# Expert weights of a decoder layer laid over partitions as 8p+k, so that a load reads 8 KB of a partition in one piece

## The chip, the cores and the metric

The kernel runs on one core of one Trainium2 chip. The metric is the device time of one execution in microseconds, the median of several runs. The engines are named as in the profile: PE is TensorE (PEld its weight loads), DVE is VectorE, ACT is ScalarE, POOL is GpSimd, SP is SyncE, whose queue (SPq) issues every DMA of this kernel. The DMA of a core is done by 16 DMA engines.

## The reference, cut to what matters

One decoder layer over 256 tokens of 1024 channels. A token mixer (sparse attention and an RWKV-7 recurrence) comes first, then a mixture of experts. Only the second half matters for the change:

```
# xt: (256 tokens, 1024 channels), after RMSNorm, scale s2 and shift sh2
# routing: best of 4 groups, best two of its 8 experts -> combine (256, 32)
def body(acc, ew):
    wg, wu, wd, cw = ew                      # (1024, 512), (1024, 512), (512, 1024), all float32
    hdn = jax.nn.silu(xt @ wg) * (xt @ wu)
    return acc + cw[:, None] * (hdn @ wd), None
acc, _ = lax.scan(body, zeros, (w_gate, w_up, w_down, combine.T))   # 32 experts
```

Each expert has 6 MB of weights, the 32 together 192 MB (here 1 MB is 1024 KB). Every expert is computed, on at most 32 of its tokens (a loop for experts with more tokens stands at the end).

## The kernel before, in words

**The weight stream.** A list `loads` holds every weight load of the program in order. For expert e it has two loads of the gate matrix (`eg`), two of the up matrix (`eu`) and then two of the down matrix of the expert before (`ed`), 1 MB each. `pump()` issues them in this order on SP's queue. Each load needs a free place of 2048 columns in SBUF: in the big tile `arena`, or in one of two tiles that appear later, `more_3006` (one place) and `more` (8192 columns, four places). `more` takes the room of the tile `split`, which holds the split operands of the output projection. Where no place is free, `pump` stops until `done()` frees one, and SP then waits for the engine that reads the old contents last.

**How rows lie.** A weight matrix is read as `(k p) n -> p k n`: row 128k+p lies on partition p in block k. A gate load of 1 MB takes four blocks, so that each partition gets four rows of 512 floats that lie 256 KB apart in memory: 4 pieces of 2 KB. A down load takes 512 of 1024 columns of four rows: again 4 pieces of 2 KB.

**The stages.** Up to about 313 us of the profile the token mixer runs. Then the output projection goes over 8 blocks of channels (line 1474 on); each block is 24 matmuls of split operands (`mm3`, lines 517 to 519), a residual add on DVE (1487), and, two blocks later, the router's sums `logits` (1462, 1464). `turn` (1470, 1471) then transposes each block on PE and copies it back to SBUF on ACT. The routing is a chain of small DVE instructions (1529 to 1579). `group` and `gather` (1593) collect the tokens of four experts at a time. For each expert `gate_up` (1618) multiplies into four row groups, ACT copies the result (1619), `hidden` (1625 to 1631) makes the SwiGLU, `down` (1637, 1638) multiplies with half of the columns of the down weights and scales on DVE, and `finish` (1658) adds to the tokens' sums in PSUM. The last expert's `finish` also adds the residual (1660) and sends the output out (1662). While the loop of expert e runs, `down` and `finish` are those of expert e-1. In the loop `done()` gives the four gate and up places back after `gate_up`, and each down place after its `down`.

Of the kernel before, what the change touches and what calls it, by code (L numbers as in the profile page):

```python
# [19 lines left out]
T = 256  # L20
# [55 lines left out]
class Arena:  # L76
    """Columns of one SBUF tile, handed out in program order from the smallest gap that holds them."""
# [11 lines left out]
    def alloc(self, cols, lo=0, hi=None, from_top=True):  # L89
        """a place that has been free for a while if there is one, in the smallest gap"""  # L90
# [65 lines left out]
def layer_kernel(tc, I, out, dbg=None):  # L156
# [17 lines left out]
    # operands in float32r: those that live to the end of the output projection, and those that live up to it  # L174
# [22 lines left out]
    # ---------------------------------------------------------------- weight stream  # L197
# [98 lines left out]
    # ---------------------------------------------------------------- small inputs  # L296
# [29 lines left out]
    # ---------------------------------------------------------------- constants  # L326
# [18 lines left out]
    def rsqrt_steps(dst, src, mul, eps, z, u):  # L345
        """dst = (src * mul + eps) ** -0.5 for a few columns, by Newton steps from a guess out of the exponent"""
# [17 lines left out]
    # ---------------------------------------------------------------- silu(c), x norm  # L364
# [24 lines left out]
    # ---------------------------------------------------------------- modulation rows  # L389
# [6 lines left out]
    def mod_cols(row, gs):  # L396
        """channel-major [128, 8] of the pairs of groups from each of gs on"""
# [11 lines left out]
    def mod_bcast(o, row, g0, mul):  # L409
        """o [128, 1024] = the row of the groups g0, g0 + 1 on every partition, times mul"""  # L410
# [10 lines left out]
    def mod_half(hf):  # L421
        """shift and scale for half of the channels, in four groups: shift and scale, even and odd blocks of rows"""
# [35 lines left out]
        # the vector engine reads one PSUM bank while the scalar engine reads the other  # L458
# [15 lines left out]
    def after_last(f, keep=True):  # L474
        """f(); with keep, the tensor engine's part of it after that of the call before"""
# [9 lines left out]
    def step(it, keep):  # L485
        """the next step of a stream"""
# [6 lines left out]
    # ---------------------------------------------------------------- input projection  # L493
# [3 lines left out]
    def split(w, p=None):  # L497
        """w (512 columns) as a float32r part and the float32r rest"""
# [11 lines left out]
    # the first blocks of weights are split before the activations are there  # L510
# [4 lines left out]
    def mm3(ps, l, r, start, stop):  # L515
        """the product of two split operands, all terms that float32 holds"""
# [4 lines left out]
    def proj_cols(key, c0, ps, last=False):  # L521
        """ps [128, T]: the columns c0 to c0 + 127 of a weight times the split activations"""
# [13 lines left out]
    def shift_mix(dst, ps, i, m=128):  # L536
        """dst = p + (previous p - p) * mu along the tokens"""
# [4 lines left out]
    def rows_part(key, hf, mp, n, fin, i0=0):  # L542
        """n blocks of columns of a weight from block 2 mp on, by half of the rows, into fin(block, their products)"""
# [74 lines left out]
    def rwkv():  # L618
        # ---------------------------------------------------------------- RWKV: decay, a, gate, kk
# [14 lines left out]
        def weave(a, b):  # L634
            """the steps of both, by turns"""
# [36 lines left out]
        # cumulative log decay within a chunk  # L672
# [1169 lines left out]
```

## Time and profile before

| | us |
|---|---|
| median of 3 runs | 833.31 (832.91 to 834.92) |
| profiled execution, first to last instruction (span) | 831.9 |
| what lies around the span, if the profiled execution took the median | 1.4 |

The profiled execution has no time of its own beside its span, so the 1.4 us are the median less the span. The page shows PE busy for 85% of the span, DVE 47%, ACT 24% and POOL 26%, and 261.46 MB moved by DMA, of which 201.3 MB (192 loads of 1 MB as above) are expert weights. A busy share is an average over stages: a matmul that waits in a full pipeline also counts as busy.

### The profile page before, as it was taken

How to read it: one execution, taken by the hardware profiler on the slowest of the kernel's cores; microseconds unless marked ns; L12 is line 12 of the kernel's file. 1: busy time of each engine (PE TensorE's matmuls, PEld its weight loads, DVE VectorE, ACT ScalarE, POOL GpSimd, SP SyncE). 2: the span in 40 equal slices, each digit the busy share in tenths (PEclk: the TensorE clock that was granted, in tenths of full speed). 3: DMA queues.
4: the chain of work that ended last, by engine and by line, in shares of the span. 5: the costliest groups of instructions: out<-in, count | busy, mean ns of one | idle time of the engine just before them, and what ended most of it. 6: DMA issues, size and time to landing. Idle time of an engine off the chain costs nothing.

```text
span 831.9 us, 12649 instructions
## 1 busy us (share of the span) xinstructions
PE 710.2 (85%) x4981; PEld 410.8 (49%) x4981; DVE 387.8 (47%) x861; ACT 201.2 (24%) x438; POOL 216.3 (26%) x251
## 2 busy tenths in 40 slices
PE   5898767899899999899996988888797897798777
PEld 2786556568789899644442332332242242242222
DVE  2577899999857674342337321221131132122113
ACT  2476512434364433211110010010010010010000
POOL 1348758323924156011110010010010001001000
PEclk9899779999999999899999899998999999999899
DMA  9994504557678579699999999999999999999993
GB/s 336 387 301 143 180 23 159 202 176 270 220 262 256 202 254 333 229 376 386 386 386 386 387 387 387 386 387 386 387 387 386 387 387 387 387 386 387 387 386 147
DMA packets 135597, 261.46 MB, mean 314 GB/s; under 512 B 7760, under 2 KB 23120, under 8 KB 133488
## 3 DMA queue, kind: packets, MB, share of 16 engines
q1 hardware_dynamic: 135536, 260.63, 86.9%
q8 instruction: 40, 0.66, 0.3%
q14 instruction: 21, 0.17, 0.1%
HBM read 259.57 MB, written 1.05 MB: 313 GB/s over the span
## 4 chain that ended last, share of the span: by engine, by line
PE 47%; DMA 26%; DVE 15%; SPq 5%; POOL 4%; issue 2%; ACT 1%; POOLq 0%; DVEq 0%
DMA arena<-in_expert_w_up_dram 16%; PE ps_e L1618 10%; DMA more<-in_expert_w_up_dram 7%; PE acc L1658 7%; SPq L280 5%; PE ps_e L1637 4%; PE ps_a L551 3%; PE ps_e L1593 2%; PE ps_g L517 2%; PE ps_e L1625 2%; PE ps_g L519 2%; PE ps_g L518 2%; DVE split L507 2%; DMA arena<-in_expert_w_down_dram 2%; DVE arena L1345 2%
## 5 line engine op out<-in xcount | busy, mean ns | idle before, releaser
L1638 DVE TENSOR_TENSOR arena<-ps_e,arena 128x512 f32<-128x512 f32 x64 | 44.3, 692 | 304.5 <-PE ps_e L1637 304.5
L1618 PE MATMUL ps_e<-arena 128*32 128x512 f32 x784 | 148.8, 661 | 33.6 <-DMA arena<-in_expert_w_up_dram 33.6
L1607 POOL TENSOR_SCALAR arena<-arena 128x128 f32<-128x128 f32 x64 | 51.6, 812 | 410.6 <-PE ps_e L1609 278.9
L1658 PE MATMUL acc<-arena 128*128 128x512 f32 x256 | 123.4, 609 | 24.9 <-DVE arena L1638 24.9
L1618 PEld LDWEIGHTS ps_e<-arena 128*32 128x32 f32 x784 | 32.2, 118 | 124.9 <-issue 65.9
L1658 PEld LDWEIGHTS acc<-arena 128*128 128x128 f32 x256 | 44.6, 192 | 83.2 <-issue 60.7
L507 DVE TENSOR_TENSOR split<-arena,split 128x512 fp32r<-128x512 f32 x84 | 67.1, 808 | 22.9 <-POOL split L504 11.2
L1619 ACT COPY arena<-ps_e 128x512 f32<-128x512 f32 x32 | 18.8, 586 | 241.0 <-PE ps_e L1618 241.0
L1618 PE MATMUL ps_e<-more,arena 128*32 128x512 f32 x240 | 68.0, 619 | 9.9 <-DMA more<-in_expert_w_up_dram 9.9
L504 POOL TENSOR_SCALAR split<-arena 128x512 fp32r<-128x512 f32 x50 | 40.3, 809 | 98.2 <-PE ps_g L518 31.8
L1637 PE MATMUL ps_e<-arena 128*32 128x512 f32 x392 | 62.8, 610 | 0.3 <-DMA arena<-in_expert_w_down_dram 0.3
L551 PE MATMUL ps_a<-split 128*128 128x256 f32 x360 | 50.0, 298 | 3.3 <-ACT split L463 1.9
L551 PEld LDWEIGHTS ps_a<-split 128*128 128x128 f32 x360 | 46.5, 200 | 9.9 <-issue 4.3
L1625 PEld LDWEIGHTS ps_e<-arena 128*128 128x128 f32 x256 | 31.1, 191 | 27.3 <-issue 21.4
L519 PE MATMUL ps_a<-split 128*128 128x256 f32 (+1 forms) x112 | 36.7, 328 | 8.8 <-DVE split L507 4.5
L506 ACT CAST split<-arena 128x512 fp32r<-128x512 f32 x60 | 36.5, 615 | 31.7 <-PE ps_g L518 18.3
L1627 ACT ACTIVATE arena<-ps_e 128x128 f32<-128x128 f32 x32 | 8.9, 278 | 141.7 <-PE ps_e L1625 141.7
L507 POOL TENSOR_TENSOR split<-arena,split 128x512 fp32r<-128x512 f32 x26 | 36.2, 1395 | 13.4 <-ACT split L506 9.6
L517 PE MATMUL ps_g<-split 128*128 128x256 f32 x128 | 38.8, 303 | 0.0
L518 PE MATMUL ps_a<-split 128*128 128x256 f32 (+1 forms) x112 | 35.6, 318 | 2.6 <-POOL split L507 1.0
L519 PE MATMUL ps_g<-split 128*128 128x256 f32 x128 | 36.4, 285 | 1.6 <-DVE split L507 1.6
L517 PE MATMUL ps_a<-split 128*128 128x256 f32 (+1 forms) x112 | 36.0, 326 | 1.8 <-ACT split L506 0.8
(349 smaller groups left out, 1246.1 us busy)
## 6 DMA issues: line engine op xcount, KB each, us to landing
arena<-in_expert_w_gate_dram SPq DMA_DIRECT2D x51, 1024.0 KB, 14.3
arena<-in_expert_w_down_dram SPq DMA_DIRECT2D x49, 1024.0 KB, 14.4
arena<-in_expert_w_up_dram SPq DMA_DIRECT2D x47, 1024.0 KB, 14.3
arena<-in_w_in_dram SPq DMA_DIRECT2D x18, 1024.0 KB, 8.7
more<-in_expert_w_up_dram SPq DMA_DIRECT2D x17, 1024.0 KB, 14.3
arena<-in_ada_w_dram SPq DMA_DIRECT2D x16, 1024.0 KB, 6.4
more<-in_expert_w_down_dram SPq DMA_DIRECT2D x15, 1024.0 KB, 14.3
more<-in_expert_w_gate_dram SPq DMA_DIRECT2D x13, 1024.0 KB, 14.4
```

Of the source, the lines that this page charges most:

```text
L280: nc.sync.dma_start(out=dst, in_=src)
L507: (nc.gpsimd if p[1] == "P" else nc.vector).tensor_sub(l, w, h.bitcast(F32))
L517: nc.tensor.matmul(ps, l[0], r[0], start=start, stop=False)
L518: nc.tensor.matmul(ps, l[0], r[1], start=False, stop=False)
L519: nc.tensor.matmul(ps, l[1], r[0], start=False, stop=stop)
L551: nc.tensor.matmul(p, a[:, kk, :], b[:, 4 * hf + kk, :], start=(i == 0 and kk == KORD[0]), stop=(i == 2 and kk == KORD[-1]))
L1607: nc.gpsimd.tensor_scalar(o4[:, a], io1[:, None, :].to_broadcast([128, 4, CAP]), rk_(a), cb(a), op0=OP.is_equal, op1=OP.mult)
L1618: nc.tensor.matmul(ps[32 * g:32 * g + 32, :], xg[:, kk, :], w[:, k, :], start=(k == 0), stop=(k == 3))
L1625: nc.tensor.matmul(ps[:, 64 * f:64 * f + 64], gu[:, 128 * f:128 * f + 128], SEL, start=True, stop=True)
L1637: nc.tensor.matmul(ps[32 * f:32 * f + 32, 0:n], hT[:, f, :], wd[:, f, :], start=True, stop=True)
L1638: nc.vector.tensor_mul(Y4b[:, s:s + n], ps[:, 0:n], gt2[0][:, s:s + n])
L1658: nc.tensor.matmul(o, stb[e % 2][:, a, :], Y4b[:, s:s + n], start=(e == 0), stop=(e == NE - 1))
```

## The change

The rows of an expert's gate and up matrices are laid over partitions as 8p+k, those of the down matrix as 4p+j. A gate or up load then reads four rows that follow each other in memory, 8 KB in one piece, on each partition; the pieces of neighbouring partitions begin 16 KB apart. A down load takes two whole rows of 1024 floats, also 8 KB in one piece. Only the two loads of the last expert's down matrix stay halves by columns (4 pieces of 2 KB).

What the new order of rows needs elsewhere:

- The channels of the tokens must lie as 8p+k. `turn` writes the transposed blocks to a new tile `h2` (2048 columns, a place of `more`) instead of back into `h`; the 8 copies on ACT have the same number of elements in another order. `h` is freed behind them.
- The scale and shift of the tokens (`s2c`, `sh2`) must follow. `reorder`, placed in the output projection behind the matmuls of block 1, does that with 16 matmuls of 8 columns, a 1024-column copy and four small instructions on DVE.
- The hidden channels must lie as 4p+j: the copy of `gate_up`'s result reads PSUM with a step of 4 elements.
- `down` takes both halves of the hidden channels at once and uses two PSUM tiles; the last expert keeps the form by columns as `down_cols`.
- The residual add of the last `finish` reads `h2` with a step of 128 elements.

```diff
-            w = I[name][0, e].rearrange("(k p) n -> p k n", p=128)
+            w = I[name][0, e].rearrange("(p k) n -> p k n", p=128)
             for i in range(2):
                 add_load((n, e, i), (4, 512), [(None, w[:, 4 * i:4 * i + 4, :])])
         if e:
-            w = I["expert_w_down"][0, e - 1].rearrange("(k p) n -> p k n", p=128)
-            for s, n in ((0, 512), (512, 512)):
-                add_load(("ed", e - 1, s), (4, n), [(None, w[:, :, s:s + n])])
+            w = I["expert_w_down"][0, e - 1].rearrange("(p k) n -> p k n", p=128)
+            for i in range(2):
+                if e < NE:
+                    add_load(("ed", e - 1, i), (2, 1024), [(None, w[:, 2 * i:2 * i + 2, :])])
+                else:
+                    add_load(("ed", e - 1, i), (4, 512), [(None, w[:, :, 512 * i:512 * i + 512])])
...
-        nc.scalar.copy(h[:, m, :], pst[:, 0:256])
+        nc.scalar.copy(h2[:, :, :, 16 * m:16 * m + 16], pst[:, 0:256].rearrange("p (a c k) -> p a k c", a=2, k=8))
+
+    blk, both = M(8), M(2, 8)
+
+    def reorder():
+        nc.vector.tensor_reduce(blk, ident.rearrange("p (m q) -> p m q", m=8), axis=AX.X, op=OP.add)
+        pick = M(8, 8, 16)
+        nc.vector.tensor_copy(pick, ident.rearrange("p (q k) -> p k q", k=8)[:, :, None, :].to_broadcast([128, 8, 8, 16]))
+        ps = PS("g")
+        for k in range(8):
+            for o, v in enumerate((sh2, s2c)):
+                nc.tensor.matmul(ps[:, 64 * o + 8 * k:64 * o + 8 * k + 8], pick[:, k].rearrange("p m q -> p (m q)"), v,
+                                 start=True, stop=True)
+        t = M(2, 8, 8)
+        pv = ps[:, 0:128].rearrange("p (o k m) -> p o k m", o=2, k=8)
+        for o in range(2):
+            nc.vector.tensor_mul(t[:, o], pv[:, o], blk[:, None, :].to_broadcast([128, 8, 8]))
+        nc.vector.tensor_reduce(both, t, axis=AX.X, op=OP.add)
+        A.free(t, blk, pick)
...
+        if j and m == 1:
+            after_last(lambda: None, False)
+            after_last(reorder)
...
+    fr.__exit__(None, None, None)
+    state["more"].append(Arena(pool(name="sb2", bufs=1).tile([128, nB], F32, name="more"), nB))
+    h2 = state["more"][-1].get(2048, from_top=False).rearrange("p (a k c) -> p a k c", a=2, k=8)
     for m in range(8):
         turn(m)
-    fr.__exit__(None, None, None)
-    state["more"].append(Arena(pool(name="sb2", bufs=1).tile([128, nB], F32, name="more"), nB))
+    A.free(h, sh2, s2c)
+    sh2, s2c = both[:, 0], both[:, 1]
...
-        nc.scalar.copy(GUb, ps)
+        nc.scalar.copy(GUb.rearrange("p (j q) -> p j q", j=4), ps.rearrange("p (q j) -> p j q", j=4))
...
-    def down(hT, wd, s, n):
+    def down(hT, wds, then=lambda i: None):
+
+        ps = [PS(), PS()]
+        for i, wd in enumerate(wds):
+            for c in range(2):
+                for j in range(2):
+                    g = 2 * (c ^ i) + j
+                    nc.tensor.matmul(ps[c][32 * g:32 * g + 32, :], hT[:, 2 * i + j, :], wd[:, j, 512 * c:512 * c + 512],
+                                     start=True, stop=True)
+            then(i)
+        for c in range(2):
+            s = slice(512 * c, 512 * c + 512)
+            nc.vector.tensor_mul(Y4b[:, s], ps[c], gt2[0][:, s])
```

**SP's queue, the loads around the routing.** The names are destination and source of a load; `more_3006` and `more` are the two late tiles. Before, the last expert loads ahead of the first expert's `gate_up` and the first ones behind it:

```order
L280 DMA arena<-in_expert_w_gate_dram 128x4x512 x2
L280 DMA more<-in_expert_w_up_dram 128x4x512 x2
L280 DMA more<-in_expert_w_down_dram 128x4x512 x2
L280 DMA arena<-in_expert_w_gate_dram 128x4x512 x2
L280 DMA arena<-in_expert_w_up_dram 128x4x512 x2
```

The same stretch of the change:

```order
L283 DMA arena<-in_expert_w_gate_dram 128x2048 x2
L283 DMA more<-in_expert_w_up_dram 128x2048 x2
L283 DMA more<-in_expert_w_down_dram 128x2048
L283 DMA arena<-in_expert_w_down_dram 128x2048
L283 DMA arena<-in_expert_w_gate_dram 128x2048 x2
```

The shape of a load goes from 4 rows of 512 on each partition to one run of 2048. `h2` has taken one of the four places of `more`, so the second down load goes to `arena` instead, into the place of the first expert's second gate load, and stands behind that expert's `gate_up`.

**PE, the output projection.** Line 1462 is the router's sums, 517 to 519 are the matmuls of split operands. Before, between blocks 1 and 2:

```order
L517 MATMUL ps_a<-split 128x256
L518 MATMUL ps_a<-split 128x256
L519 MATMUL ps_a<-split 128x256
L1462 MATMUL ps_r<-arena 128x36 x2
L517 MATMUL ps_a<-split 128x256
```

The place of the change where the 16 matmuls stand (lines 517 to 519 are 520 to 522 here):

```order
L521 MATMUL ps_a<-split 128x256
L522 MATMUL ps_a<-split 128x256
L1485 MATMUL ps_g<-arena 128x8 x16
L520 MATMUL ps_a<-split 128x256
L521 MATMUL ps_a<-split 128x256
```

They stand between the last product of block 1 and the second half of block 2, 12 matmuls ahead of the router's first sums; nothing else on PE moves in this stage.

**PE, the end of the program.** Line 1618 is `gate_up` of the last expert, 1637 `down`, 1625 `hidden`, 1609 the scatter weights, 1658 `finish`. Before:

```order
L1618 MATMUL ps_e<-arena 32x512 x16
L1637 MATMUL ps_e<-arena 32x512 x4
L1625 MATMUL ps_e<-arena 128x64 x4
L1609 MATMUL ps_e<-arena 128x128 x2
L1637 MATMUL ps_e<-arena 32x512 x4
L1658 MATMUL acc_3389<-arena 128x512
L1658 MATMUL acc_3391<-arena 128x512
L1637 MATMUL ps_e<-arena 32x512 x4
```

The change:

```order
L1645 MATMUL ps_e<-arena 32x512 x16
L1667 MATMUL ps_e<-arena 32x512 x8
L1652 MATMUL ps_e<-arena 128x64 x4
L1636 MATMUL ps_e<-arena 128x128 x2
L1699 MATMUL acc_3410<-arena 128x512
L1699 MATMUL acc_3412<-arena 128x512
L1678 MATMUL ps_e<-arena 32x512 x4
```

The eight `down` matmuls of expert 30 stand together now, ahead of `hidden`; the number of matmuls from `gate_up` to the end is the same.

## Rows read from the trace of the kernel before

**Rows 1.** The page, part 2: DMA share and rate in 40 equal slices

```profile
DMA  9994504557678579699999999999999999999993
GB/s 336 387 301 143 180 23 159 202 176 270 220 262 256 202 254 333 229 376 386 386 386 386 387 387 387 386 387 386 387 387 386 387 387 387 387 386 387 387 386 147
```

**Rows 2.** Busy time by stage, one stage of the experts; last three columns: clock, DMA share, GB/s

```profile
430.00:808.00 378.00, 310.88 (x1710) 116.38 (x1702) 96.35 (x204) 35.92 (x91) 38.70 (x48) 0.95 1.05 387
```

**Rows 3.** The chain that ended last, in order of time: start, length, what

```profile
375.24 3.57 PE ps_e L1593 x32
...
388.79 3.57 PE ps_e L1618 x32
...
398.78 3.57 PE ps_e L1618 x32
...
529.73 3.19 PE ps_e L1618 x25
...
808.75 4.62 PE ps_e L1618 x25
```

**Rows 4.** Timeline of SP's queue around the routing: start, length, issue

```profile
334.19 0.93 SPq L280 DMA_DIRECT2D more<-in_expert_w_up_dram  x2
335.17 1.61 SPq L280 DMA_DIRECT2D more<-in_expert_w_down_dram  x2
352.35 0.92 SPq L280 DMA_DIRECT2D arena<-in_expert_w_gate_dram  x2
```

**Rows 5.** DMA issues in 220 to 345 us: expert loads, KB each, us to landing

```profile
arena<-in_expert_w_gate_dram SPq DMA_DIRECT2D x8, 1024.0 KB, 6.4
arena<-in_expert_w_up_dram SPq DMA_DIRECT2D x5, 1024.0 KB, 5.6
arena<-in_expert_w_down_dram SPq DMA_DIRECT2D x4, 1024.0 KB, 10.5
...
more<-in_expert_w_up_dram SPq DMA_DIRECT2D x3, 1024.0 KB, 8.0
...
more<-in_expert_w_down_dram SPq DMA_DIRECT2D x2, 1024.0 KB, 11.8
```

**Rows 6.** DMA share and rate in 340 to 360 us, 40 slices of 0.5 us

```profile
DMA  9999999999999930000000000009489999999999
GB/s 401 414 406 406 401 397 393 389 389 385 381 381 389 356 115 0 0 0 0 0 0 0 0 0 0 0 8 102 164 332 401 389 381 373 397 389 344 414 414 393
```

**Rows 7.** Busy time by stage, two short stages; last three columns: clock, DMA share, GB/s

```profile
90.00:93.00 3.00, 0.95 (x6) 0.54 (x5) 3.00 (x5) 1.47 (x3) 3.00 (x3) 1.00 1.02 431
94.00:96.00 2.00, 0.23 (x1) 0.23 (x2) 2.00 (x3) 0.92 (x2) 2.00 (x2) 0.71 1.05 404
```

**Rows 8.** DMA issues in 86 to 98 us

```profile
arena<-in_ada_w_dram SPq DMA_DIRECT2D x2, 1024.0 KB, 5.8
arena<-in_w_in_dram SPq DMA_DIRECT2D x1, 1024.0 KB, 9.1
```

**Rows 9.** The chain again, in the output projection

```profile
320.88 0.37 PE ps_r L1462 x4
...
336.23 0.58 PE ps_r L1464 x6
```

**Rows 10.** Groups by line (page, part 5): mean of one in ns, idle before

```profile
L1638 DVE TENSOR_TENSOR arena<-ps_e,arena 128x512 f32<-128x512 f32 x64 | 44.3, 692 | 304.5 <-PE ps_e L1637 304.5
```

**Rows 11.** Timeline of ACT and DVE in the routing

```profile
338.86 0.65 ACT L1471 COPY arena<-ps_g 128x256 f32<-128x256 f32 x2 [0.25 <-PE ps_g L1470]
...
340.43 0.53 ACT L1573 ACTIVATE arena<-arena 128x32 f32<-128x32 f32 x2
...
341.35 0.19 DVE L1575 CUSTOM_DVE_ANT_0 arena<-arena 128x32 f32<-128x32 f32 x1 [0.34 <-POOL arena L1567]
```

**Rows 12.** Timeline of the end

```profile
821.67 1.07 PE L1637 MATMUL ps_e<-arena 128*32 128x512 f32 x8
...
826.40 0.69 DVE L1660 TENSOR_TENSOR arena<-acc,arena 128x512 f32<-128x512 f32 x1 [0.17 <-PE acc L1658]
```

More of the change, by code (lines that the diff above doesn't have):

```diff
@@ L1592, in gather @@
                 for a in range(2):
-                    nc.tensor.matmul(ps[:, n * kk:n * kk + n], h[:, 2 * k2 + kk, 128 * a:128 * a + 128], oh(a), start=(a == 0),
+                    nc.tensor.matmul(ps[:, n * kk:n * kk + n], h2[:, a, 2 * k2 + kk, :], oh(a), start=(a == 0),
                                      stop=(a == 1))
@@ L1631, in hidden, with down_cols @@
         nc.vector.tensor_mul(hT, pv[:, :, 1, :], sg[:, 0])
-    def down(hT, wd, s, n):
+    def down(hT, wds, then=lambda i: None):
[10 more added lines that the diff above has]
+            nc.vector.tensor_mul(Y4b[:, s], ps[c], gt2[0][:, s])
+    def down_cols(hT, wd, s):
         ps = PS()
         for f in range(4):
-            nc.tensor.matmul(ps[32 * f:32 * f + 32, 0:n], hT[:, f, :], wd[:, f, :], start=True, stop=True)
-        nc.vector.tensor_mul(Y4b[:, s:s + n], ps[:, 0:n], gt2[0][:, s:s + n])
+            nc.tensor.matmul(ps[32 * f:32 * f + 32, :], hT[:, f, :], wd[:, f, :], start=True, stop=True)
+        nc.vector.tensor_mul(Y4b[:, s:s + 512], ps, gt2[0][:, s:s + 512])
     pctx.__exit__(None, None, None)
@@ L1659, in finish @@
             if e == NE - 1:
-                nc.vector.tensor_add(y[:, a, s:s + n].rearrange("p (k n) -> p k n", n=128), o.rearrange("p (k n) -> p k n", n=128),
-                                     h[:, s // 128:(s + n) // 128, 128 * a:128 * a + 128])
+                nc.vector.tensor_add(y[:, a, s:s + n].rearrange("p (c k) -> p c k", k=8), o.rearrange("p (c k) -> p c k", k=8),
+                                     h2[:, a, :, s // 8:(s + n) // 8].rearrange("p k c -> p c k"))
                 nc.sync.dma_start(out=out[0, 128 * a:128 * a + 128, s:s + n], in_=y[:, a, s:s + n])
@@ L1687, in layer_kernel @@
             break
-        for c in (0, 512) if e else ():
-            down(hTb, need(("ed", e - 1, c)), c, 512)
-            done(("ed", e - 1, c))
+        if e:
+            down(hTb, [need(("ed", e - 1, i)) for i in range(2)], lambda i: done(("ed", e - 1, i)))
         hidden(hTb)
@@ L1699, in layer_kernel @@
             overflow_tables(nc, ovm, PS(), sel, rk, comb, ones, io)
-    parts = [(e, c) for e in (NE - 2, NE - 1) for c in (0, 512)]
     last[0] = None
-    for i, (e, c) in enumerate(parts):
-        after_last(lambda: down(hTb if e < NE - 1 else hT2, need(("ed", e, c)), c, 512))
-        done(("ed", e, c))
-        if i == 0:
-            after_last(lambda: hidden(hT2))
-            e = NE - 1
-            after_last(lambda: scatter_weights(stb[e % 2], o4b, lambda a: rk[:, a, e:e + 1], lambda a: comb[:, a, e:e + 1]))
-        else:
-            after_last(lambda: finish(*parts[i - 1], 512))
-    after_last(lambda: finish(*parts[-1], 512))
+    e = NE - 1
+    after_last(lambda: down(hTb, [need(("ed", e - 1, i)) for i in range(2)], lambda i: done(("ed", e - 1, i))))
+    after_last(lambda: hidden(hT2))
+    after_last(lambda: scatter_weights(stb[e % 2], o4b, lambda a: rk[:, a, e:e + 1], lambda a: comb[:, a, e:e + 1]))
+    after_last(lambda: finish(e - 1, 0, 512))
+    for i in range(2):
+        after_last(lambda: down_cols(hT2, need(("ed", e, i)), 512 * i))
+        done(("ed", e, i))
+        after_last(lambda: finish(*((e, 0) if i else (e - 1, 512)), 512))
+    after_last(lambda: finish(e, 512, 512))
     ovr, ovw, ovi = ovm[6:]
@@ L1723, in layer_kernel @@
             for t, n in zip(wts, ("expert_w_gate", "expert_w_up", "expert_w_down")):
[L1724 removed]
+                nc.sync.dma_start(out=t, in_=I[n][0, ds(eid, 1)].rearrange("o (p k) n -> p (o k) n", p=128))
             nc.vector.tensor_copy(rw[:, 0], ovr[:, :, ds(i, 1)].rearrange("p a o -> p (a o)"))
@@ L1731, in layer_kernel @@
             hidden(hTb)
-            for c in (0, 512):
-                down(hTb, wts[2][:, :, c:c + 512], c, 512)
+            down(hTb, [wts[2][:, 2 * j:2 * j + 2, :] for j in range(2)])
             scatter_weights(stb[0], o4b, lambda a: rw[:, 0, a:a + 1], lambda a: rw[:, 1, a:a + 1])
```

1 line of the change is left out of this document (removed).

## The prediction, written before the result was known

> **What bounds the kernel now.** I first read the rate of the DMA over the span [rows 1]. Up to slice 17 it moves between 23 and 387 GB/s; in slices 19 to 39, some 437 us, it stands at 386 or 387. The row of the stage from 430 us on says the same: 387 GB/s at a DMA share of 1.05, so the engines' transfers lie end to end [rows 2]. Then the chain in order of time [rows 3]. Around 390 us its pieces are PE's: the `gate_up` of one expert starts at 388.79, the next at 398.78, so PE needs 9.99 us for an expert, and 3.57 us more at every fourth for the `gather` (line 1593), 10.9 us on average. Later each long piece ahead of a `gate_up` is the DMA of its last up load. `gate_up` starts at 529.73 and, 17 experts on, at 808.75: 279.0 / 17 = 16.41 us for six loads, **2.735 us for a load of 1 MB**. The DMA is thus slower than PE by half, and the end is set by how many loads are left when the expert stage begins, and by the pace of one.
>
> When does the stage begin? SP's queue shows the last loads ahead of it at 334.19 and 335.17, and the next at 352.35 [rows 4]; the issues of 220 to 345 us count 8 + 5 + 4 + 3 + 2 = 22 expert loads [rows 5]. These fill every free place. The DMA then has nothing to do: its rate is zero from about 347.5 us on until the first `gate_up` gives places back at 352.35 [rows 6]. So whatever delays that `gate_up` delays the whole stream behind it, one for one, and loads that come earlier ahead of 347 us win nothing.
>
> The sum of before: 192 loads, of which the last four are the down matrices of experts 30 and 31. Up to the last up load 188 - 22 = 166 loads come after 352.35. 166 x 2.735 = 454.0; it lands at 808.75, 456.4 us later, so 2.4 us are the first transfer's start. From there to the end of the span 831.9 - 808.75 = 23.15 us, PE's chain through the last expert; 1.4 us lie around the span: 833.3, the median.
>
> **The change part by part.**
>
> *The pace of a load.* This trace has loads in pieces of 8 KB already: at 87 us two loads of `in_ada_w`, 2048 columns of one row for each partition, with a load of `in_w_in` in 2 KB pieces (4 rows of 512) behind them [rows 8]. In the 3 us in which only the first two run, the rate is 431 GB/s; in the 2 us of the third it is 404 [rows 7]. Two readings: taken as it is, 431 against the 387 of the long stage; or, since 2 KB pieces also run at 404 in so short a stretch and at 387 in a long one (the slices from 340 us on fall the same way, from 414 to 381), the long stage keeps the ratio, 387 x 431 / 404 = 413. I take the middle, **422**: both ends come from one pair of rows, and neither is nearer. A load then takes 2.735 x 387 / 422 = 2.508 us (2.456 to 2.563).
>
> The Trainium skill, "DMA: Bandwidth & Descriptors", section "Why small descriptors are slow (HBM only)", says that every packet costs some 3 cycles beside its 32-byte beats. A piece of 2 KB would then go from 67 to 64.75 cycles for each 2 KB, 3.5%, and the whole would come to about 824 us. The pair of rows shows 6.7% between the two sizes, so the trace does not agree with so small a cost.
>
> *One load more.* `h2` takes one of the four places of `more`, and `h`'s room, freed, makes no other place: SP's order shows the second down load of expert 2 behind the first `gate_up`. 21 loads lie ahead, 167 follow: 2.5 us.
>
> *`reorder`.* PE sits in the output projection without a gap and on the chain. Of the nearest row, the router's sums, four entries (two matmuls of 36 columns) take 0.37 us, and six of one column 0.58 [rows 9]: 0.19 us a matmul whatever the columns, two entries each. 16 x 0.19 = **3.0 us** on the path. On DVE a copy of 1024 columns is about twice a 512-column instruction of 692 ns [rows 10], 1.4 us, placed in the branch projection, ahead of what makes the splits that PE waits for; between nothing and 1.4 I take 0.5. The four small DVE instructions lie beside PE's 3 us. Together 3.5 us (bounds 2.5 to 5.5).
>
> *`turn`.* Eight copies on ACT, 0.65 us a pair, the last ending at 339.5; then the exponentials (0.53), which end at 340.96, and DVE takes their result at 341.35 [rows 11]: 0.4 us of cover, and then the routing, on the path, waits. Nothing in the trace shows a copy with this order of elements. The number of elements is the same; I take nothing, and as the other bound 2 us (each copy longer by 0.25 us), which the 5.5 above includes.
>
> *The order of `gate_up`'s copy, `down`, `finish`.* Up to 430 us PE's work is hidden behind the DMA's backlog, later behind its pace: 10.9 us of work against 15.05. Uncovered is only the end. There the same matmuls stand in another order, and the last add on DVE (0.69 us) reads with a step: nothing, or one more 0.69 [rows 12]. The last four loads come 2 x 2.51 + 2 x 2.735 = 10.5 us after the last up load, and PE wants the last of them at 821.67 - 808.75 = 12.9 us: 2.4 us of cover; I leave 23.15 as it is.
>
> **The sum.** 352.35 + 3.5 = 355.85; + 2.4 + 167 x 2.508 (418.8) = 777.05; + 23.15 = 800.2 of span; + 1.4 = **801.6, said as 802**. The bounds of the pace give 793 and 811, those of the rest move this by 1 down and 3 up: 792 to 814.
>
> **The rivals.**
>
> *The long pieces help only up to the short-stretch rate.* If what slows 2 KB pieces from 404 to 387 in a long run is their number alone, and nothing is won beyond, the pace is 2.735 x 387 / 404 = 2.62 us and the time 801.6 + 18.7 = 820. For it: 404 is the one rate that 2 KB pieces have reached. Against: the 431 beside it. This is also where the skill's rule above ends.
>
> *The memory sets the pace, not the pieces.* 387 stands to within one GB/s for 437 us, as a fixed limit would. Then 167 x 2.735 = 456.7, and with the 3.5 us of `reorder` and the added load the time is 839.5: slower. It decides where the pace stays over (454.0 - 3.5) / 167 = 2.698 us, a rate under 392. Against: 404 and 431 in the same trace, and a share of 1.05 in the DMA's own rows. The skill's "DMA: Bandwidth & Descriptors", section "Where 436 GB/s comes from", holds that memory binds loads at about 358 GB/s a core; the 387 of this trace is above that already, so it can't be the limit here.
>
> *The new addresses collide.* The pieces of neighbouring partitions begin 16 KB apart, a power of two, where those of `in_ada_w` are 24 KB apart; the trace has no long load with such a step. At 360 GB/s a load takes 2.94 us, and the time is 874.
>
> *PE becomes the bound.* It needs 10.9 us against 15.05 an expert. Only a clock that falls by a quarter closes that; the stage shows 0.95 [rows 2]. Then some 833.
>
> **How the numbers follow.** My forecast 0.66, the short-stretch rate 0.16, the memory's limit 0.09, PE as the bound or a mixture that eats the gain 0.05, collisions 0.04. The range for 8 in 10 reaches from 789 (a pace a little under the lower bound) to 823, with the first rival in it; the likeliest case alone has 792 to 814. A difference of 0.3% (2.5 us) is about what a measurement of this kernel can tell from none: under 830.8 is faster, with the first two cases and a part of the mixture, 0.86; same 0.04; slower 0.10, the memory's limit and the collisions less a little.
>
> **What the profile would show.** Rate of the long stage: 413 to 431 says the step on the pace is right, 404 the first rival, 387 the second, less the third. The share of DMA should be near 1 again. Six loads: about 15.05 us between two `gate_up` of the DMA-bound stretch. The gap of the DMA ahead of the first `gate_up` should grow (the loads end earlier), and the first issue behind it should come at 355 to 358. The chain's late pieces should still be up loads; if they are PE's, PE has become the bound. Wrong would make me above all a rate that falls over a long run more for long pieces than for short ones, or copies of `turn` far longer than 0.35 us.

## The result, and the profile after

| | before | after |
|---|---|---|
| median | 834.12 us (832.91 to 839.86) | 805.76 us (803.52 to 808.79, 4 runs) |
| profiled execution: time | not given | 806.51 us |
| its span | 831.9 us | 804.7 us |

The ratio is 0.9654 with a 95% interval of 0.9601 to 0.9706: faster, 28 us. The forecast was 802 us in a range of 789 to 823.

The changed kernel's page, part 2 (40 slices of the span) and its packets, answers to [rows 1]; the last line is the packets of before:

```profile
DMA  9995414456788566649999999999999999999994
GB/s 334 386 302 182 157 53 131 144 211 213 260 283 286 198 235 248 231 165 407 421 421 420 422 421 421 419 421 421 421 421 420 423 420 421 421 420 422 420 418 155
DMA packets 62636, 261.45 MB, mean 325 GB/s; under 512 B 7760, under 2 KB 23120, under 8 KB 36208
...
DMA packets 135597, 261.46 MB, mean 314 GB/s; under 512 B 7760, under 2 KB 23120, under 8 KB 133488
```

The same megabytes go in fewer than half of the packets, and the long stage, which stood at 386 or 387 GB/s, stands at 418 to 423. The window of that stage (PE, PEld, DVE, ACT and POOL busy, then PE's granted clock, DMA share, GB/s) answers to [rows 2]:

```profile
430.00:780.00 350.00, 295.58 (x1776) 120.30 (x1774) 92.50 (x209) 38.14 (x96) 40.85 (x50) 0.99 1.01 421
```

The chain in order of time (start, length, what), which answers to [rows 3]:

```profile
507.47 19.81 DMA arena<-in_expert_w_up_dram
527.33 3.19 PE ps_e L1645 x25
...
567.52 19.70 DMA arena<-in_expert_w_up_dram
587.27 3.19 PE ps_e L1645 x25
```

And PE's timeline at the end, the last `gate_up` behind its up load:

```profile
782.79 3.19 PE L1645 MATMUL ps_e<-arena 128*32 128x512 f32 x25 [1.43 <-DMA arena<-in_expert_w_up_dram]
```

From 527.33 to 782.79 are 17 experts again: 255.46 / 17 = 15.03 us for six loads, 2.505 us for one. The late pieces of the chain are still up loads, so the DMA is still the bound. They are longer than before (19.8 us from issue to landing, where the chain of before has some 14.5), although a load takes less: by the pace of each, an estimate, 19.8 / 2.505 = 7.9 loads stand in the queue when one is issued, and 14.5 / 2.735 = 5.3 before.

SP's queue around the routing answers to [rows 4], the DMA's rate from 330 to 380 us (slices of 1.25 us) to [rows 6]:

```profile
337.15 0.33 SPq L283 DMA_DIRECT2D arena<-in_expert_w_gate_dram  x1
341.82 0.80 SPq L283 DMA_DIRECT2D more<-in_expert_w_up_dram  x2
342.67 0.42 SPq L283 DMA_DIRECT2D more<-in_expert_w_down_dram  x1
360.44 0.33 SPq L283 DMA_DIRECT2D arena<-in_expert_w_down_dram  x1
```

```profile
GB/s 0 177 354 302 7 0 105 256 419 59 151 321 433 426 413 406 347 33 0 0 0 0 0 0 0 170 354 419 419 419 426 387 387 393 400 419 433 419 426 439
```

Only one down load goes to `more`, and the next stands behind the first `gate_up`, as the order of instructions had shown. It is issued at 360.44, 8.1 us later than before. The gap with a rate of zero has grown from some 5 us to 9 us.

| term | forecast | profiled execution |
|---|---|---|
| first issue behind the gap | 355.85 | 360.44 |
| from it to the last up load's landing, 167 loads | 421.2 | 782.79 - 360.44 = 422.35 |
| from there to the end of the span | 23.15 | 804.7 - 782.79 = 21.9 |
| around the span | 1.4 | 806.51 - 804.7 = 1.8 |
| sum | 801.6 | 806.5 |

So the term that carries the gain is right to 1.2 us, and the start of the stage is off by 4.6 us.

Why is it late? The chain of waits through the output projection (L1485 is `reorder`, L1465 the router's sums, L1620 the `gather`, L520 and L521 matmuls of split operands of 256 columns):

```profile
318.66 3.60 PE ps_g L1485 x32
...
324.38 0.21 PE ps_a L520
...
325.02 0.54 PE ps_r L1465 x4
...
325.76 0.12 PE ps_a L521
...
328.51 0.37 PE ps_r L1465 x4
```

A matmul of the same shape takes 0.21 us in one place and 0.12 us in another. The windows of these microseconds say why (columns as above); the last line is the trace of before:

```profile
313.00:315.00 2.00, 0.89 (x6) 0.49 (x5) 1.12 (x2) 1.14 (x2) 2.00 (x2) 1.00 0.45 78
315.00:317.00 2.00, 2.00 (x10) 2.00 (x11) 1.69 (x3) 0.62 (x1) 0.53 (x2) 0.51 0.91 344
317.00:319.00 2.00, 2.00 (x15) 2.00 (x13) 0.31 (x2) 0.81 (x2) 1.03 (x1) 0.64 0.97 356
...
323.00:325.00 2.00, 2.00 (x12) 2.00 (x11) 0.00 (x0) 0.00 (x0) 0.10 (x1) 0.50 1.01 426
...
312.00:314.00 2.00, 0.89 (x5) 0.48 (x5) 1.09 (x2) 1.14 (x2) 2.00 (x2) 1.00 0.40 99
```

PE waits for the splits in 313 to 315 (busy 0.89 of 2.00 us); from 315 on its granted clock is 0.51, the 1.2 GHz level, then full for some 4 us while most of `reorder` runs, then 0.50 again to about 325.5. In the trace of before PE waits as much (busy 0.89 us of 312 to 314), but the clock stays at 1.00 in every window up to 328 us. The 8.1 us come apart as:

- 1.0 already there before any changed instruction (the chain passes the same wait for a split at 313.80 instead of 312.77);
- 3.6 for `reorder`, most of it at full clock;
- 3.0 for the matmuls at the lower clock, half of them ahead of `reorder` (314.86 to 318.66 takes 3.80 us, where the same 17 matmuls take 2.29 before) and half behind it (322.26 to 325.57 takes 3.31 us in the place of 1.81);
- 0.4 in the `gather` (6.52 us in the place of 6.12).

### The profile page after: what moved, and what is told of

Read it like the earlier page. It is cut to its first block, busy times and chain, and to the rows that moved or that the text cites. A ratio compares the mean times of both kernels' runs of the same rounds, so it can differ in the third digit from the quotient of the medians.

```text
span 804.7 us, 12679 instructions
## 1 busy us (share of the span) xinstructions
PE 694.5 (86%) x5013; PEld 418.0 (52%) x5013; DVE 382.7 (48%) x866; ACT 201.4 (25%) x438; POOL 216.4 (27%) x251
## 2 busy tenths in 40 slices
DMA packets 62636, 261.45 MB, mean 325 GB/s; under 512 B 7760, under 2 KB 23120, under 8 KB 36208
## 4 chain that ended last, share of the span: by engine, by line
PE 44%; DMA 32%; DVE 16%; POOL 4%; issue 2%; ACT 1%; DVEq 0%; SPq 0%; POOLq 0%
DMA arena<-in_expert_w_gate_dram 10%; DMA arena<-in_expert_w_up_dram 10%; PE ps_e L1645 7%; PE acc L1699 6%; DMA arena<-in_expert_w_down_dram 5%; PE ps_a L554 3%; PE ps_e L1620 3%; PE ps_e L1667 3%; PE ps_g L520 3%; DMA more<-in_expert_w_up_dram 3%; DMA more<-in_expert_w_gate_dram 2%; PE ps_g L522 2%; PE ps_g L521 2%; DVE split L510 2%; PE ps_e L1652 2%
## 5 line engine op out<-in xcount | busy, mean ns | idle before, releaser
L1645 PE MATMUL ps_e<-arena 128*32 128x512 f32 x832 | 134.5, 601 | 16.7 <-DMA arena<-in_expert_w_up_dram 16.7
L1699 PE MATMUL acc<-arena 128*128 128x512 f32 x256 | 119.9, 611 | 31.6 <-DVE arena L1672 31.6
L1699 PEld LDWEIGHTS acc<-arena 128*128 128x128 f32 x256 | 46.7, 193 | 98.2 <-DVE arena L1672 50.0
L1655 DVE TENSOR_SCALAR arena<-arena 128x128 f32<-128x128 f32 x32 | 7.2, 226 | 171.9 <-ACT arena L1654 171.6
L1667 PE MATMUL ps_e<-arena 128*32 128x512 f32 x400 | 62.2, 601 | 0.5 <-DMA arena<-in_expert_w_down_dram 0.5
L1672 DVE TENSOR_TENSOR arena<-ps_e,arena 128x512 f32<-128x512 f32 x62 | 40.3, 683 | 45.6 <-PE ps_e L1667 45.5
L1645 PE MATMUL ps_e<-more,arena 128*32 128x512 f32 x192 | 57.5, 606 | 2.7 <-DMA more<-in_expert_w_up_dram 2.7
L522 PE MATMUL ps_a<-split 128*128 128x256 f32 (+1 forms) x112 | 37.4, 334 | 8.1 <-DVE split L510 4.2
L1620 PEld LDWEIGHTS ps_e<-arena,more 128*128 128x128 f32 x256 | 33.4, 206 | 16.7 <-ACT arena L1637 6.9
L1620 PE MATMUL ps_e<-arena,more 128*128 128x128 f32 x256 | 35.7, 294 | 7.0 <-DVE arena L1692 5.6
L520 PE MATMUL ps_g<-split 128*128 128x256 f32 x128 | 39.0, 305 | 0.0
L521 PE MATMUL ps_a<-split 128*128 128x256 f32 (+1 forms) x112 | 36.4, 325 | 2.6 <-POOL split L510 1.0
## 6 DMA issues: line engine op xcount, KB each, us to landing
arena<-in_expert_w_up_dram SPq DMA_DIRECT2D x52, 1024.0 KB, 19.8
arena<-in_expert_w_gate_dram SPq DMA_DIRECT2D x52, 1024.0 KB, 19.8
arena<-in_expert_w_down_dram SPq DMA_DIRECT2D x52, 1024.0 KB, 19.8
more<-in_expert_w_up_dram SPq DMA_DIRECT2D x12, 1024.0 KB, 19.8
more<-in_expert_w_down_dram SPq DMA_DIRECT2D x12, 1024.0 KB, 19.8
```

Of the source, the lines that this page charges most:

```text
L520: nc.tensor.matmul(ps, l[0], r[0], start=start, stop=False)
L521: nc.tensor.matmul(ps, l[0], r[1], start=False, stop=False)
L522: nc.tensor.matmul(ps, l[1], r[0], start=False, stop=stop)
L1620: nc.tensor.matmul(ps[:, n * kk:n * kk + n], h2[:, a, 2 * k2 + kk, :], oh(a), start=(a == 0), stop=(a == 1))
L1645: nc.tensor.matmul(ps[32 * g:32 * g + 32, :], xg[:, kk, :], w[:, k, :], start=(k == 0), stop=(k == 3))
L1667: nc.tensor.matmul(ps[c][32 * g:32 * g + 32, :], hT[:, 2 * i + j, :], wd[:, j, 512 * c:512 * c + 512], start=True, stop=True)
```

## The experiments

All are compared with the kernel before on the same chip, which had medians of 832.92 us beside e1 to e4 and 832.6 beside e5 to e8. The medians of e3, e4 and e5 can't be told apart, and the intervals of e6 and e7 overlap.

| run | what | median, us | ratio to before, 95% interval |
|---|---|---|---|
| e1 | whole change, pieces of 2 KB | 843.33 (839.54 to 843.97) | 1.0121 [1.0090, 1.0151] |
| e2 | whole change, pieces of 4 KB | 822.03 (819.64 to 823.68) | 0.9851 [0.9820, 0.9882] |
| e3 | `reorder` in 8 matmuls | 802.07 (800.07 to 809.79) | 0.9642 [0.9605, 0.9678] |
| e4 | `reorder` behind the routing's matmuls | 802.44 (799.21 to 803.93) | 0.9618 [0.9589, 0.9647] |
| e5 | the change again | 803.05 (802.02 to 805.53) | 0.9631 [0.9584, 0.9678] |
| e6 | e3, the lost place regained | 797.85 (797.05 to 801.50) | 0.9567 [0.9528, 0.9606] |
| e7 | e6, pieces of 16 KB from expert 6 on | 794.06 (792.82 to 798.29) | 0.9533 [0.9496, 0.9570] |
| e8 | e6, pieces of 16 KB everywhere | 805.78 (804.63 to 807.99) | 0.9668 [0.9622, 0.9715] |

**e1 and e2: is it the length of a piece?** Both keep the other parts of the change (h2, reorder, the strided copies, one load more behind the first `gate_up`) and alter which rows a load takes. In e1 a gate or up load takes every second row of a partition, so that its pieces are 2 KB, and all down loads go by columns (with `down_cols`, so this part of the change is not in e1); in e2 it takes every second pair of rows, of gate, up and down alike. The rows' order in `gate_up` and `down` follows. First e1, then e2:

```diff
-            w = I[name][0, e].rearrange("(p k) n -> p k n", p=128)
-                add_load((n, e, i), (4, 512), [(None, w[:, 4 * i:4 * i + 4, :])])
+            w = I[name][0, e].rearrange("(p k i) n -> p i k n", p=128, i=2)
+                add_load((n, e, i), (4, 512), [(None, w[:, i])])
```

```diff
+            w = I[name][0, e].rearrange("(p a i c) n -> p i a (c n)", p=128, i=2, c=2)
+                add_load((n, e, i), (2, 1024), [(None, w[:, i])])
```

> The whole change with its order of rows (8p+k, 4p+j), reorder, h2 and all, but each load takes every second row of a partition (gate, up) or half of the columns (down, as before), so that pieces are 2 KB again. My theory, the length of a piece sets the pace: 387 GB/s, 2.735 us a load, 167 loads behind the first gate_up; with the first issue at 360.4 as in the profile of the change the time is about 844 (839 if the clock holds in the output projection). Rival, the order of the addresses or the new queueing sets the pace: 421 GB/s stays, about 806.

> The same with pieces of 4 KB (gate and up: two rows, a gap of two, two rows; down: two rows of 4 KB). My theory, a fixed cost for each piece: 4 pieces a partition cost 2.735 us, 1 costs 2.505, so each piece costs 0.077 and 2 pieces 2.582 us, 410 GB/s; time about 819. Rivals: a threshold between 2 and 4 KB (421 GB/s, about 806) or between 4 and 8 KB (387 GB/s, about 844).

The windows of 500 to 700 us, of e1, of e2 and of the change:

```profile
500.00:700.00 200.00, 163.78 (x894) 61.60 (x898) 43.52 (x93) 19.04 (x48) 19.32 (x24) 0.96 1.05 387
```

```profile
500.00:700.00 200.00, 167.20 (x965) 65.78 (x965) 46.17 (x105) 20.70 (x53) 22.55 (x28) 0.99 1.03 409
```

```profile
500.00:700.00 200.00, 169.32 (x1016) 67.79 (x1014) 44.48 (x101) 21.45 (x54) 22.30 (x28) 0.99 1.01 421
```

With 2 KB the rate is back at 387 to the digit, and the kernel is 1.2% slower than before: about that is what the rest of the change costs. e1's profiled execution, the fastest of its six, took 839.54 us, with its first issue behind the gap 3.5 us later than before and one load more:

```profile
355.84 0.54 SPq L280 DMA_DIRECT2D arena<-in_expert_w_down_dram  x1
```

This is the second rival's sum (839.5) for a pace that stays; the median is 4 us above it. e2 runs at 409 GB/s, where a fixed cost for each piece had given 410 and a threshold 421 or 387; its time is 3 us over the expected 819, and its profile shows the lower clock from 317 to 331 us. The packets go with the pieces: 135597 in e1, 86956 in e2, 62636 in the change. So the gain comes from the length of the pieces, and 4 KB lies between.

**e3: 8 matmuls instead of 16.** Scale and shift are first copied side by side, then one matmul of 16 columns replaces two of 8.

```diff
+        v2 = M(2, 8)
+        for o, v in enumerate((sh2, s2c)):
+            nc.vector.tensor_copy(v2[:, o], v)
         for k in range(8):
-            for o, v in enumerate((sh2, s2c)):
-                nc.tensor.matmul(ps[:, 64 * o + 8 * k:64 * o + 8 * k + 8], pick[:, k].rearrange("p m q -> p (m q)"), v,
+            nc.tensor.matmul(ps[:, 16 * k:16 * k + 16], pick[:, k].rearrange("p m q -> p (m q)"), v2.rearrange("p o m -> p (o m)"),
```

> The change with reorder's 16 matmuls of 8 columns made 8 of 16 columns, at the same place. My theory, a matmul costs the same whatever its columns: reorder takes 1.8 us on PE in place of 3.6, the time falls by 1.8 to about 804. If the clock fell at 315 to 325 us because of these matmuls it falls for a shorter time or not at all, and the time is 801 to 803; if it fell for another reason, 804 and the clock is low at the same place. Rival, PE waits for the splits there anyway: no difference, 806.

Chain and SP's queue of e3:

```profile
315.95 1.69 PE ps_g L1487 x16
```

```profile
354.40 0.33 SPq L283 DMA_DIRECT2D arena<-in_expert_w_down_dram  x1
```

Half the matmuls, half the time: between 8 and 16 columns the number of matmuls counts, not the columns. The clock is 1.00 from 304 to 321 us here and stays so, and the first issue comes 2.05 us later than before, not 8.1. The median is what was expected where the clock holds; it is 3.7 us under that of the change and 1.0 under that of e5, the same program as the change, with intervals that overlap: the 1.8 us are shown in `reorder`'s row, not in the time of the kernel.

**e4: `reorder` off the projection.** It runs behind the routing's matmuls, where PE was thought idle; POOL makes its table of 1024 columns in the room of `Y4b`.

```diff
-            after_last(reorder)
...
+    pick = Y4b.rearrange("p (k m q) -> p k m q", k=8, m=8)
+    nc.gpsimd.tensor_copy(pick, ident.rearrange("p (q k) -> p k q", k=8)[:, :, None, :].to_broadcast([128, 8, 8, 16]))
...
+        if q == 0:
+            reorder()
```

> The change with reorder (8 matmuls) moved behind the routing's own matmuls, where PE waits for DVE, its selecting table made by POOL in a buffer that the experts use later; 22 loads then stand ahead of the first gate_up again. My theory: 3.6 us of PE leave the path, one load (2.5 us) leaves the stage behind, some 1 us comes back since DVE waits for the 8 matmuls in the routing: about 801, first issue behind the gap near 357. If the fall of the clock came from reorder it is gone too: 798. Rival, POOL's copy of 1024 columns delays the merge of the branches by 2 us or more: 803 and over.

```profile
345.01 3.58 PE ps_e L1484 x16
```

```profile
342.32 0.33 SPq L283 DMA_DIRECT2D arena<-in_expert_w_up_dram  x1
342.70 0.90 SPq L283 DMA_DIRECT2D more<-in_expert_w_down_dram  x2
358.94 0.80 SPq L283 DMA_DIRECT2D arena<-in_expert_w_gate_dram  x2
```

It won nothing on e3: behind PE's idle time in the routing the clock is 0.50 (345 to 349 us), the same 8 matmuls take 3.58 us, and they stand on the chain. Its profile is also late from the token mixer on (the last wait for a split is passed at 315.91, in e3 at 312.61), so not all of 358.94 is due to the move. POOL's copy, the rival's reason, takes 2.23 us at 287.4, but this profile is some 4 us behind e3's at 183 us already. And 22 loads lie ahead of the first `gate_up` again: a load goes to `arena` at 342.32, and both down loads to `more`. Here `Y4b` lies elsewhere than in the change. That put the prediction's account of the lost load in doubt, which e6 tests.

**e5: the change once more.** No edit; the question is whether the clock's fall belongs to the 16 matmuls.

> The changed kernel once more, nothing altered, on another chip and day of the clock. If TensorE's fall to 1.2 GHz in the output projection comes from reorder's 16 small matmuls, it shows again between 313 and 325 us, and the first load behind the routing is issued at 358 to 361 us, time 804 to 808. If the fall is a chance of one execution, the stretch stands at a granted clock of 1.00, the first issue comes at 355.5 to 357.5, and the time is nearer 803. The rate of 500 to 700 us is 421 GB/s either way.

Windows of e5:

```profile
313.00:315.00 2.00, 1.10 (x5) 0.70 (x5) 1.32 (x2) 1.14 (x2) 2.00 (x2) 1.00 0.51 90
...
319.00:321.00 2.00, 2.00 (x19) 2.00 (x19) 0.00 (x0) 0.00 (x0) 1.35 (x2) 1.00 0.97 352
321.00:323.00 2.00, 2.00 (x12) 2.00 (x13) 0.64 (x3) 0.00 (x0) 0.00 (x0) 0.62 1.01 418
323.00:325.00 2.00, 2.00 (x11) 2.00 (x11) 1.18 (x2) 0.42 (x1) 1.29 (x2) 0.52 1.00 422
```

The clock falls once, behind `reorder`, and not ahead of it as in the first profile. So the first sign of the expectation came, a fall again and a first issue at 358 to 361, while the median, 803.05, is nearer the other case. The first issue comes at 358.03 and the last up load lands at 780.00: 421.97 us for the 167 loads, the same pace. The two profiles of one program differ by 2.4 us in the start of the stage; the sum is 358.03 + 421.97 + 21.7 + 1.8 = 803.5.

e1, which has the same 16 matmuls at full clock (3.47 us from 315.45 on), falls behind them too:

```profile
319.00:321.30 2.30, 2.30 (x14) 2.30 (x13) 0.60 (x3) 0.00 (x0) 0.04 (x1) 0.53 1.05 399
```

**e6: the place that was lost.** The program's own list of places shows that in the change and in e3 `Y4b` (1024 columns) is laid into the first half of the 2048 columns that `h` leaves, and in e4 elsewhere. e6 hands out `GUb`, `Y4b` and `stb` first, so that they fill smaller gaps and `h`'s room stays whole.

```diff
+    GUb = ME(512)
+    Y4b = ME(1024)
+    stb = [ME(2, 128), ME(2, 128)]
     hTb = ME(4, CAP)
     SEL = ME(64)
-    stb = [ME(2, 128), ME(2, 128)]
-    GUb = ME(512)
-    Y4b = ME(1024)
```

> The 8-matmul form of reorder, and the small tiles behind turn handed out in another order (GUb and Y4b first), so that the 1024-column tile Y4b no longer stands in the 2048 columns that h has left. My theory: the load lost ahead of the first gate_up is lost to Y4b, not to h2; 22 loads then lie ahead instead of 21, 166 follow, and one load of 2.505 us is won: 802.1 - 2.5 = 799.6. Rival: the load into h's place waits for turn's last transposes and holds up the three behind it on SP's queue, which then land no earlier than needed: no gain, 802.

SP's queue of e6, and PE's timeline ahead of `reorder` (L1487):

```profile
345.12 0.33 SPq L283 DMA_DIRECT2D arena<-in_expert_w_up_dram  x1
345.50 0.90 SPq L283 DMA_DIRECT2D more<-in_expert_w_down_dram  x2
357.56 0.80 SPq L283 DMA_DIRECT2D arena<-in_expert_w_gate_dram  x2
```

```profile
313.92 0.28 PE L522 MATMUL ps_a<-split 128*128 128x256 f32 x1
314.04 0.28 PE L520 MATMUL ps_a<-split 128*128 128x256 f32 x1
...
315.99 0.41 PE L521 MATMUL ps_a<-split 128*128 128x256 f32 x1
316.20 0.41 PE L522 MATMUL ps_a<-split 128*128 128x256 f32 x1
316.42 3.43 PE L1487 MATMUL ps_g<-arena 128*128 128x16 f32 x16
```

The load goes into `h`'s place at 345.12, all 22 lie ahead, and the last up load lands at 777.51: 419.95 us after the first issue, where the change needs 422.35. That is one load of 2.4 us. The median is 4.2 us under e3's (expected 2.5); the executions of each spread by more than the difference. The rival fell: the load into `h`'s place does wait and holds up the two behind it (345.50, where the change issues its down load at 342.67), but that costs nothing, since the DMA's rate still falls to zero ahead of 357.56. The rows of PE also say something of the clock: matmuls that started 0.12 us apart at 314 us start 0.21 us apart at 316, ahead of `reorder`, and with 8 matmuls in it. So a fall ahead of `reorder`, here and in the first profile of the change, is not made by it.

**e7 and e8: does 16 KB give more?** A gate, up or down matrix becomes one load of 2 MB, 16 KB in one piece on each partition: in e7 from expert 6 on (`E16` is 6), in e8 for all; the last down matrix stays in halves.

```diff
-            for i in range(2):
+            if e >= E16:
+                add_load((n, e), (8, 512), [(None, w)])
+            for i in range(2 if e < E16 else 0):
                 add_load((n, e, i), (4, 512), [(None, w[:, 4 * i:4 * i + 4, :])])
```

> As the run before, but from expert 6 on a gate, an up or a down matrix is one load of 2 MB with 16 KB in one piece on each partition. If each piece costs a fixed 0.077 us of a 1 MB load (2.735, 2.582 and 2.505 us with 4, 2 and 1 pieces), half a piece gives 2.467 us for 1 MB, 427.5 GB/s; 154 of the 166 MB are loaded so: 154 x 0.038 = 5.9 us less, 793.7. Rival: 8 KB is where it ends (421 GB/s is the limit of the engines or the memory): 799.6. Second rival: places of 4096 columns come free later, the DMA waits, its share falls under 1, and the time is over 802.

> As e7, with loads of 2 MB for all experts. Only 16 MB instead of 22 then fit ahead of the first gate_up, since places of 4096 columns are rarer: 172 MB follow. By the fixed cost of a piece: 172 x 2.467 = 424.3 us against 166 x 2.505 = 415.8 of e6, 8.5 more: 808. By a limit at 421 GB/s: 172 x 2.505 = 430.9, 15 more: 814.7. If the loads ahead did not matter, it would be as fast as e7.

Windows of e7, then of e8:

```profile
380.00:400.00 20.00, 20.00 (x137) 7.96 (x136) 6.11 (x12) 3.18 (x8) 4.77 (x6) 1.00 0.99 398
...
500.00:700.00 200.00, 162.02 (x986) 66.29 (x988) 45.34 (x99) 20.20 (x51) 20.95 (x26) 0.97 1.01 428
```

```profile
500.00:700.00 200.00, 165.74 (x1000) 68.64 (x993) 47.69 (x103) 21.42 (x54) 22.19 (x28) 0.97 1.01 428
```

The rate is 428 GB/s in both (expected 427.5), so 421 is no limit of the memory or the engines. Here the load grows with the piece, from 1 to 2 MB; no run has long pieces in small loads, so that the step comes from the piece and not from the number of loads is likely by e1 and e2, not shown. e7 has the lowest median, 794.06 us, and it meets the expected 793.7 by two misses that cancel: e6, on which it stands, was 1.8 us faster than expected, and by the medians the step to 16 KB gave 3.8 us instead of 5.9. The profiles, in which the spread of the earlier stages drops out, have 5.3: from the first issue to the last up load e7 takes 768.31 - 353.62 = 414.69 us, e6 419.95. Part of what is missing is in the window from 380 to 400 us, where the rate is 398; that places of 4096 columns come free later there is argued, not tested. e8 has the same rate and is 11.7 us slower than e7, 2 us under the 808 that the cost of a piece had given. The last `gate_up` behind its up load, of e7 and of e8:

```profile
768.31 3.63 PE L1664 MATMUL ps_e<-arena 128*32 128x512 f32 x28 [1.96 <-DMA arena<-in_expert_w_up_dram]
...
780.26 3.63 PE L1645 MATMUL ps_e<-arena 128*32 128x512 f32 x28 [2.91 <-DMA arena<-in_expert_w_up_dram]
```

In e8 only 16 MB fit ahead of the first `gate_up` instead of 22, and SP then waits until it gives room back:

```profile
340.34 11.78 SPq L281 DMA_DIRECT2D arena<-in_expert_w_up_dram  x2
353.52 0.33 SPq L281 DMA_DIRECT2D arena<-in_expert_w_gate_dram  x1
```

6 MB more in the stage are 6 x 2.45 = 14.7 us, of which 12.0 show at the last up load. Some 2 us come back since the first load behind the wait goes out at about 351.8 (340.34 + 11.78, less the 0.3 of an issue), ahead of e7's 353.62, and some 0.5, an estimate, by the 12 MB of the stage that e7 still takes in pieces of 8 KB.

## Why the prediction was right, and where it was off

*The bound and the sum's form: right.* The stage still runs at a DMA share of 1.01, the chain's late pieces are still up loads, and the time is first issue + loads x pace + tail.

*The pace: right, 422 forecast and 421 measured (2.508 and 2.505 us a load).* That it came out so closely is luck: it was a middle between two readings, and neither of these held: 431 was not kept over the long stretch, and the ratio of 431 to 404 was too small (6.7%, where the long stage shows 421 / 387 = 8.8%). What the runs show is a cost for each piece. 1 MB (1,048,576 bytes) at 387, 409, 421 and 428 GB/s is 2.709, 2.564, 2.491 and 2.450 us, with 4, 2, 1 and half a piece on a partition: 0.073, 0.073 and 0.082 us for each further piece. (By the chain a load takes 0.6 to 1% more than the rate gives, and the three pieces between 2.735 and 2.505 us cost 0.077 each.) Worked back to no pieces, 2.491 - 0.073 = 2.418 us would be 434 GB/s, an estimate from these rows.

The Trainium skill's rule weighed ahead ("DMA: Bandwidth & Descriptors", "Why small descriptors are slow (HBM only)") has the right form, a fixed cost for a packet, but the size does not agree: 3 cycles on 64 are 4.7% of a 2 KB piece, an estimate (6% with the 32 bytes of descriptor that the section also counts), and the rows give 0.073 / (2.418 / 4) = 12%. In the same page of the Trainium skill the section "Where 436 GB/s comes from" gives 435 GB/s for the ports into SBUF, and the 434 worked back here lies near that; its other figure, that the memory binds loads at about 358 GB/s a core, does not hold in these runs, where one core at work loads at 387 to 428.

*The first rival (404) and the second (387) fell* by the rate alone; e1 shows what the second would have looked like. (That 404 was the one rate reached with 2 KB pieces was misread: [rows 6] have half microseconds of such loads at up to 414.) *The third (collisions by a step of 16 KB) fell too:* the whole stage has that step, at 421 GB/s. *The fourth* (PE as the bound) fell with a clock of 0.99 in the stage.

*One load more: the count was right, the reason wrong.* The prediction said that `h2` takes one of the four places of `more`, and `h`'s room, freed, makes no other place. `h`'s room is a place; in the change `Y4b` was laid into it. e6 puts `Y4b` elsewhere and has the load back.

*`reorder`: 3.0 us forecast on PE, 3.60 measured in the change and 3.47 in e5;* e3 with half the matmuls takes 1.69. The 0.5 us for DVE's copy can't be told from the spread of the earlier stages (over the ten profiles the last wait for a split is passed between 312.11 and 315.91 us): in e3 the first issue is 2.05 us late with 1.69 of `reorder`.

*The start of the stage is the term that was mis-sized: 3.5 us forecast (bounds 2.5 to 5.5), 8.1 measured.* Apart from 1.0 us of spread and 0.6 more in `reorder`, the clock did it, 3.0 us in the first profile. The prediction considered the clock only in the expert stage. It should have asked it of the projection too, the last stretch that PE bounds, since that delays the stream one for one. Of ten profiles with this projection the clock falls between 313 and 331 us in five (the change, e1, e2, e5, e6) and in the other five not (before, e3, e4, e7, e8). In all ten PE waits about as long for the first splits, 1.1 to 1.4 us.

Two kinds of fall have to be kept apart. The one ahead of `reorder` (the change, e2, e6) is not made by it, and it is not fixed by the program: e6 and e7 are the same program up to there, as are the change and e5, and yet they differ. Behind `reorder` the clock is at the lower level in all four profiles that have its 16 matmuls (the change, e1, e2, e5), in three of them by a new fall, in e2 by the first one going on; with 8 matmuls it is so only in e6, where it had fallen before, and not in e3, e7 and e8; with none in this stage (before, e4) it never falls. So that the 16 small matmuls bring the clock down behind them fits every profile, though ten are few and no run was made to test it. What decides the fall ahead of them stays open.

*`turn`: nothing, as said.* The last copies of `turn` and the exponentials on ACT, which answer to [rows 11]:

```profile
346.49 0.65 ACT L1474 COPY more<-ps_g 128x256 f32<-128x256 f32 x2 [0.25 <-PE ps_g L1473]
...
348.11 0.53 ACT L1600 ACTIVATE arena<-arena 128x32 f32<-128x32 f32 x2
```

A pair takes 0.65 us in either order of elements.

*The last add: not nothing, but the other bound.* With the step of 128 elements each of the four adds takes about 1.0 us, where [rows 12] have 0.69, and they now end the chain:

```profile
797.33 3.84 DVE L1701 TENSOR_TENSOR arena<-acc,more 128x512 f32<-128x512 f32 x4 [0.33 <-PE acc L1699]
```

The last of them ends at 801.17; behind the last matmul, which ends at 799.86, one add of 0.69 would have ended some 0.6 us earlier.

*The gap of the DMA grew, but not as said.* The loads ahead of it were to end earlier; they end later (352 instead of 347.5 us), because those into `more` can only be issued when the projection has ended, and that was late itself: 341.82 in the place of 334.19. It costs nothing, since the DMA then waits for the first `gate_up` anyway.

*The tail* was 21.9 us, 1.2 shorter than left standing, a sum of terms that the prediction did not have. The last `gate_up` takes 3.19 us where it took 4.62 [rows 3], at a granted clock of 1.00 instead of 0.69 (e1, with pieces of 2 KB, has 4.60): 1.4 less. PE waits 0.50 us for the second down load of expert 30, since the eight `down` matmuls now stand ahead of `hidden`; the prediction had looked at the cover of the last load alone. Another 0.44 us pass ahead of `down_cols`. The adds cost the 0.6. From the end of the last add to the end of the span it is 3.5 us instead of 4.8; why is open.

## What to carry to other kernels

Where a stage runs at a DMA share of 1 and its rate stands still, look at the length of the pieces before calling it the memory's limit: from 2 to 4, 8 and 16 KB this one went from 387 to 409, 421 and 428 GB/s. Larger loads need larger places, though, and when they cost loads ahead of the stage (e8), the gain is gone; long pieces only where the places are turned over anyway (e7) kept both. What prepares such a change is paid in full where it stands on the chain that starts the stream: count its instructions (8 matmuls cost half of 16), ask what the clock does there, and look at what the allocator does with the room that it frees.

## What the runs showed of the hardware that was not expected

- Each piece on a partition costs a 1 MB load 0.073 us between pieces of 2, 4 and 8 KB; from 8 to 16 KB, where the load grows too, the rate rises by as much again for the half piece (0.082 for a whole one).
- In the same program PE's granted clock falls from 1.00 to 0.50 in one execution and not in another, behind a wait of 1.1 to 1.4 us, and stays there while PE is busy without a gap (e6: 2.00 of 2.00 us from 315 to 323, at 0.50). In e2 this lasted from 317 to 331 us and doubled `reorder`, which took 6.63 us.
- PE's small matmuls also took twice as long at the lower clock (8 of them 1.69 us in e3, 3.58 in e4), so their price is not a fixed delay.
- An add of 512 columns on DVE took 1.0 us in the place of 0.69 where one operand was read with a step of 128 elements from SBUF; ACT's copies that write in another order took the same 0.65 us a pair.
